# Kurtosis of 1024 rows: loads of changing size, a larger first result batch, another split of the last fourth powers, and the last results with one row per partition

## Chip, cores, metric

The kernel runs on one core of a Trainium2 chip. The metric is the device time of one execution in microseconds. "The span" is the length of a profiled execution; the measured time is about 1.7 us longer (100.4 and 102.1 us for the kernel before). A packet is one entry of the trace's DMA list, here one contiguous piece of a row. A semaphore is a counter on which an engine waits.

## The reference

```python
x = np.random.randn(1024, 8192).astype(np.float32)
mean = np.mean(x, axis=-1, keepdims=True)
std = np.std(x, axis=-1, keepdims=True)
z = (x - mean) / (std + 1e-8)
return (np.mean(z ** 4, axis=-1) - 3).astype(np.float32)     # 1024 results, 4 KB
```

The input is 33.55 MB and is read once. The output is 4 KB.

## The kernel before

The rows go in 16 groups of 64. A row fills two partitions, so a group is a tile of 128 partitions x 4096 values (2 MB). For each group the TensorE transposes and adds 32 blocks (`turn`), the VectorE (DVE) adds the two halves (`reduce`), the TensorE makes the mean of each partition (`mean`), and the ScalarE (ACT) squares the centred values (`square`). The fourth powers are split between ACT (512 columns) and DVE (3584); in the last group 2304 and 1792. The SyncE (SP) issues all loads and stores.

```python
def load(i):                                   # 4 loads of 512 KB a group, all issued by SP
    ...
    for c in range(0, W, CHUNK):               # CHUNK = 1024, W = 4096
        nc.sync.dma_start(out=xt[:, c:c + CHUNK], in_=src[:, c:c + CHUNK])

def second_moment(b):                          # n groups of batch b, R = 64 rows each
    p2 = psfin.tile([n, R], f32, name="p2")    # one partition per group, 64 results in it
    nc.tensor.matmul(p2, lhsT=sa[:, 0:n], rhs=sel, start=True, stop=True)
    ...                                        # rec = 1/p2; rec2 = -rec*rec

def finish(b, rec2):
    ...                                        # p4: the same with the fourth powers (2 matmuls)
    nc.vector.tensor_mul(kr, p4, rec2)
    nc.vector.tensor_scalar_add(kr, kr, -3.0)
    dst = out[b[0] * R:(b[0] + n) * R].rearrange("(g r) -> g r", r=R)
    nc.sync.dma_start(out=dst, in_=kr)         # n packets of 256 B

for i in range(GROUPS):
    turn(i); reduce(i); mean(i); square(i)     # (one line here, four in the kernel)
    if i >= 1: fourth_dve(i - 1, ACT_S4)
    if i < L:  fourth_act(i, ACT_S4)
    if i == LAG_BATCH + 1: finish(batches[0], second_moment(batches[0]))
rec2 = second_moment(batches[1]); rec2l = second_moment(batches[2])
fourth_act(L, LAST_ACT_S4); fourth_dve(L, LAST_ACT_S4)
finish(batches[1], rec2); finish(batches[2], rec2l)
```

The batches are groups 0 to 11, 12 to 14, and 15.

Of the kernel before, what the change touches and what calls it, by code (L numbers as in the profile page):

```python
# [1 line left out]

# [4 lines left out]

f32 = mybir.dt.float32
bf16 = mybir.dt.bfloat16
AO = mybir.AluOpType  # L10
AF = mybir.ActivationFunctionType
P = 128

K = 2
GROUPS = 16
CHUNK = 1024
SLOTS = 12
ACT_S4 = 512
LAST_ACT_S4 = 2304
LAG_BATCH = 12  # L20


@with_exitstack
def kernel(
    ctx: ExitStack,
    tc: tile.TileContext,
    x: bass.AP,
    out: bass.AP,
):
    nc = tc.nc  # L30
    n_rows, n_cols = x.shape
    R = P // K
    W = n_cols // K
    assert n_rows == GROUPS * R
    neg_inv_n = -1.0 / float(n_cols)
    AX = mybir.AxisListType.X

    xpool = ctx.enter_context(tc.tile_pool(name="xpool", bufs=SLOTS))
    const = ctx.enter_context(tc.tile_pool(name="const", bufs=1))
    small = ctx.enter_context(tc.tile_pool(name="small", bufs=4))  # L40
    fin = ctx.enter_context(tc.tile_pool(name="fin", bufs=3))
    psum = ctx.enter_context(tc.tile_pool(name="psum", bufs=2, space=bass.MemoryType.PSUM))
    psfin = ctx.enter_context(tc.tile_pool(name="psfin", bufs=1, space=bass.MemoryType.PSUM))
    ctx.enter_context(tc.manual_schedule())

    warm = const.tile([P, 1], f32, name="warm")
    nc.vector.memset(warm, 0.0)  # L47
    nc.scalar.activation(out=warm, in_=warm, func=AF.Square)  # L48

    ident = const.tile([P, P], f32, name="ident")  # L50
    nc.gpsimd.memset(ident, 1.0)
    nc.gpsimd.affine_select(
        out=ident, in_=ident, pattern=[[-1, P]], base=0,
        channel_multiplier=1, compare_op=AO.is_equal, fill=0.0)
    negcol = const.tile([P, 1], f32, name="negcol")
    nc.gpsimd.memset(negcol, neg_inv_n)

    sel = const.tile([P, R], f32, name="sel")
    nc.gpsimd.memset(sel, neg_inv_n)
    nc.gpsimd.affine_select(  # L60
        out=sel, in_=sel, pattern=[[-K, R]], base=0,
        channel_multiplier=1, compare_op=AO.is_ge, fill=0.0)
    nc.gpsimd.affine_select(
        out=sel, in_=sel, pattern=[[K, R]], base=K - 1,
        channel_multiplier=-1, compare_op=AO.is_ge, fill=0.0)
    one = const.tile([1, 1], f32, name="one")
    nc.gpsimd.memset(one, 1.0)

    batches = [list(range(LAG_BATCH)), list(range(LAG_BATCH, GROUPS - 1)), [GROUPS - 1]]
    where = {}  # L70
    for b in batches:
        n = len(b)
        sa = const.tile([P, 2 * n], f32, name=f"sa{b[0]}")
        sd = const.tile([P, n], f32, name=f"sd{b[0]}")
        for j, i in enumerate(b):
            where[i] = (j, n, sa, sd)

    xts = {}
    tpss = {}
    reds = {}  # L80
    mpss = {}

    def load(i):
        xt = xpool.tile([P, W], f32, name="xt")
        xts[i] = xt
        src = x[i * R:(i + 1) * R, :].rearrange("r (k w) -> (r k) w", k=K)
        for c in range(0, W, CHUNK):
            nc.sync.dma_start(out=xt[:, c:c + CHUNK], in_=src[:, c:c + CHUNK])  # L88

    def turn(i):  # L90
        tps = psum.tile([P, P], f32, name="tps")
        tpss[i] = tps
        for c in range(0, W, P):
            nc.tensor.matmul(tps, lhsT=xts[i][:, c:c + P], rhs=ident,  # L94
                             start=c == 0, stop=c == W - P, is_transpose=True)

    def reduce(i):
        red = small.tile([P, P], f32, name="red")
        reds[i] = red
        nc.vector.tensor_reduce(  # L100
            out=red.rearrange("p (r k) -> p r k", k=K),
            in_=tpss[i].rearrange("p (r k) -> p r k", k=K).unsqueeze(2).to_broadcast([P, R, K, K]),
            op=AO.add, axis=AX)

    def mean(i):
        mps = psum.tile([P, 1], f32, name="mps")
        nc.tensor.matmul(mps, lhsT=reds[i], rhs=negcol, start=True, stop=True)  # L107
        nmu = small.tile([P, 1], f32, name="nmu")
        nc.scalar.copy(nmu, mps)  # L109
        mpss[i] = nmu  # L110

    def square(i):
        j, n, sa, sd = where[i]
        nc.scalar.activation(out=xts[i], in_=xts[i], func=AF.Square, bias=mpss[i],  # L114
                             accum_out=sa[:, j:j + 1])

    def fourth_act(i, c):
        j, n, sa, sd = where[i]
        nc.scalar.activation(out=xts[i][:, :c], in_=xts[i][:, :c], func=AF.Square,  # L119
                             accum_out=sa[:, n + j:n + j + 1])  # L120

    def fourth_dve(i, c):
        j, n, sa, sd = where[i]
        nc.vector.tensor_tensor_reduce(  # L124
            out=xts[i][:, c:], in0=xts[i][:, c:], in1=xts[i][:, c:], scale=1.0, scalar=0.0,
            op0=AO.mult, op1=AO.add, accum_out=sd[:, j:j + 1])


    def second_moment(b):
        j, n, sa, sd = where[b[0]]  # L130
        p2 = psfin.tile([n, R], f32, name="p2")
        nc.tensor.matmul(p2, lhsT=sa[:, 0:n], rhs=sel, start=True, stop=True)  # L132
        rec = fin.tile([n, R], f32, name="rec")
        nc.vector.reciprocal(rec, p2)  # L134
        rec2 = fin.tile([n, R], f32, name="rec2")
        nc.vector.scalar_tensor_tensor(  # L136
            out=rec2, in0=rec, scalar=-1.0, in1=rec, op0=AO.mult, op1=AO.mult)
        return rec2

    def finish(b, rec2):  # L140
        j, n, sa, sd = where[b[0]]
        p4 = psfin.tile([n, R], f32, name="p4")
        nc.tensor.matmul(p4, lhsT=sa[:, n:2 * n], rhs=sel, start=True, stop=False)  # L143
        nc.tensor.matmul(p4, lhsT=sd, rhs=sel, start=False, stop=True)  # L144
        kr = fin.tile([n, R], f32, name="kr")
        nc.vector.tensor_mul(kr, p4, rec2)  # L146
        nc.vector.tensor_scalar_add(kr, kr, -3.0)  # L147
        dst = out[b[0] * R:(b[0] + n) * R].rearrange("(g r) -> g r", r=R)
        nc.sync.dma_start(out=dst, in_=kr)

    L = GROUPS - 1
    for i in range(GROUPS):
        load(i)
    for i in range(GROUPS):
        turn(i)
        reduce(i)
        mean(i)
        square(i)
        if i >= 1:
            fourth_dve(i - 1, ACT_S4)  # L160
        if i < L:
            fourth_act(i, ACT_S4)
        if i == LAG_BATCH + 1:
            finish(batches[0], second_moment(batches[0]))
    rec2 = second_moment(batches[1])
    rec2l = second_moment(batches[2])
    fourth_act(L, LAST_ACT_S4)
    fourth_dve(L, LAST_ACT_S4)
    finish(batches[1], rec2)
    finish(batches[2], rec2l)  # L170


# [1 line left out]
_INS = ['x']  # L174
_OUTS = [((1024,), 'float32')]


# [23 lines left out]
```

## Time and profile before

| | before |
|---|---|
| time, median of 4 runs | 102.06 us (102.01 to 102.17) |
| span | 100.4 us |
| group 15 complete in SBUF | 87.36 us |
| square of group 15 starts | 89.72 us |
| last DVE operation ends | 98.07 us |
| last store: issued, landed | 98.09, 99.26 us |

"Complete" and "landed" are from the trace's list of semaphore increments: each of the up to 16 DMA engines of a transfer adds one when its share is done, and the last counts. The prediction shows the lines of the page and the timeline.

### The profile page before, as it was taken

Reading aid. Unit: us, or ns where it says so; the run is one execution under the profiler, and the core shown is the slowest. Engines: PE = TensorE matmul, PEld = TensorE weight load, DVE = VectorE, ACT = ScalarE, POOL = GpSimd, SP = SyncE. Lnnn points to the kernel's source line nnn. Section 1 sums busy time; section 2 is a strip of 40 time slices with the busy share of each in tenths; the row PEclk is TensorE's granted clock in tenths of the full one; section 3 lists DMA queues with packets and bytes.
Section 4 is the critical chain, followed back from the end, with each engine's and each line's share of the span. In section 5 each row is a group of like instructions: output and inputs, shape, how many; then the busy total and the mean of one; then the engine's idle time right before and its main releaser. Section 6 shows DMA issues by size and latency. Waiting matters only on the chain.

```text
span 100.4 us, 1513 instructions
## 1 busy us (share of the span) xinstructions
PE 73.0 (73%) x562; PEld 63.2 (63%) x562; DVE 69.2 (69%) x61; ACT 77.7 (77%) x82; POOL 1.3 (1%) x11
## 2 busy tenths in 40 slices
PE   0099797979597978888797979797979796940320
PEld 0099697967475858676777767676767695930210
DVE  0000104989792969696979787888878799979770
ACT  5000089999996798989797999898989897999910
POOL 5000000000000000000000000000000000000000
PEclk9999999999999999999999999999999999999555
DMA  1999999999999999999999999999999999100000
GB/s 59 284 374 372 418 418 415 415 405 408 408 413 406 408 415 406 405 410 415 405 410 415 405 410 410 406 405 408 411 410 408 408 408 371 64 0 0 0 0 3
DMA packets 9255, 33.65 MB, mean 335 GB/s; under 512 B 1056, under 2 KB 1056, under 8 KB 9248
## 3 DMA queue, kind: packets, MB, share of 16 engines
q1 hardware_dynamic: 9248, 33.56, 84.7%
q8 instruction: 4, 0.07, 0.3%
q14 instruction: 3, 0.02, 0.1%
HBM read 33.55 MB, written 0.00 MB: 334 GB/s over the span
## 4 chain that ended last, share of the span: by engine, by line
DMA 77%; DVE 8%; ACT 8%; PE 1%; issue 1%; SPq 1%; ACTq 0%; DVEq 0%
DMA xt<-in_x_dram 77%; ACT xt L114 8%; DVE xt L124 6%; DVE rec L134 1%; SPq L88 1%; ACT xt L119 1%; DVE kr L146 1%; DVE red L100 0%; PE p L132 0%; PE p L143 0%; PE mps L107 0%; DVE rec L136 0%; DVE kr L147 0%; PE p L144 0%; ACTq L114 0%
## 5 line engine op out<-in xcount | busy, mean ns | idle before, releaser
L94 PE MATMUL tps<-ident,xt 128*128 128x128 f32 x512 | 67.1, 285 | 8.1 <-DMA xt<-in_x_dram 8.0
L94 PEld LDWEIGHTS tps<-ident,xt 128*128 128x128 f32 x512 | 59.3, 148 | 13.8 <-DMA xt<-in_x_dram 7.7
L124 DVE CUSTOM_DVE_ANT_0 xt<-xt 128x3584 f32<-128x3584 f32 (+1 forms) x16 | 60.3, 3766 | 0.2 <-ACT xt L114 0.2
L114 ACT ACTIVATE xt<-xt,nmu 128x4096 f32<-128x4096 f32 x16 | 59.5, 3718 | 0.9 <-ACT nmu L109 0.3
L100 DVE TENSOR_REDUCE red<-tps 128x128 f32<-128x256 f32 x16 | 6.8, 424 | 26.4 <-PE tps L94 26.4
L109 ACT COPY nmu<-mps 128x1 f32<-128x1 f32 x16 | 2.5, 157 | 15.8 <-PE mps L107 15.6
L107 PEld LDWEIGHTS mps<-negcol,red 128*128 128x128 f32 x32 | 4.8, 188 | 13.3 <-ACT xt L114 9.0
L107 PE MATMUL mps<-negcol,red 128*128 128x1 f32 x32 | 5.7, 247 | 9.9 <-DVE red L100 8.7
L119 ACT ACTIVATE xt<-xt 128x512 f32<-128x512 f32 (+1 forms) x16 | 11.6, 723 | 0.5
L132 PE MATMUL p<-sel,sa 128*12 128x64 f32 (+2 forms) x6 | 0.9, 244 | 3.9 <-ACT xt L114 3.9
L143 PE MATMUL p<-sel,sa 128*12 128x64 f32 (+2 forms) x6 | 1.1, 273 | 2.6 <-DVE kr L146 2.6
L119 ACT ACTIVATION_READ_ACCUMULATOR xt<-xt 128x1 f32 x16 | 3.0, 186 | 0.0
L114 ACT ACTIVATION_READ_ACCUMULATOR xt<-xt,nmu 128x1 f32 x16 | 2.9, 184 | 0.0
L132 PEld LDWEIGHTS p<-sel,sa 128*12 128x12 f32 (+2 forms) x6 | 0.3, 84 | 4.1 <-ACT xt L114 4.1
L143 PEld LDWEIGHTS p<-sel,sa 128*12 128x12 f32 (+2 forms) x6 | 0.5, 101 | 2.9 <-issue 2.9
L134 DVE RECIPROCAL rec<-p 12x64 f32<-12x64 f32 (+2 forms) x3 | 1.6, 543 | 0.5 <-PE p L132 0.5
L48 ACT ACT_TABLE_LOAD x1 | 1.3, 1283 | 0.8 <-PEq L185 0.8
L124 DVE DVE_READ_ACCUMULATOR2_ANT sd<- 128x1 f32 x16 | 1.3, 82 | 0.0
L144 PE MATMUL p<-sel,sd 128*12 128x64 f32 (+2 forms) x6 | 1.1, 281 | 0.0
L146 DVE TENSOR_TENSOR kr<-p,rec 12x64 f32<-12x64 f32 (+2 forms) x3 | 0.6, 211 | 0.7 <-PE p L144 0.6
L136 DVE SCALAR_TENSOR_TENSOR rec<-rec 12x64 f32<-12x64 f32 (+2 forms) x3 | 0.6, 213 | 0.1
L47 DVE MEMSET warm<- 128x1 f32 x1 | 0.1, 59 | 0.9 <-PEq L185 0.9
(14 smaller groups left out, 3.1 us busy)
## 6 DMA issues: line engine op xcount, KB each, us to landing
xt<-in_x_dram SPq DMA_DIRECT2D x64, 512.0 KB, 10.2
out_dram<-kr SPq DMA_DIRECT2D x1, 3.0 KB
out_dram<-kr SPq DMA_DIRECT2D x1, 0.8 KB
out_dram<-kr SPq DMA_DIRECT2D x1, 0.2 KB
```

The lines of the kernel that those rows point to most:

```text
L48: nc.scalar.activation(out=warm, in_=warm, func=AF.Square)
L94: nc.tensor.matmul(tps, lhsT=xts[i][:, c:c + P], rhs=ident, start=c == 0, stop=c == W - P, is_transpose=True)
L100: nc.vector.tensor_reduce(out=red.rearrange("p (r k) -> p r k", k=K), in_=tpss[i].rearrange("p (r k) -> p r k", k=K).unsqueeze(2).to_broad ...
L107: nc.tensor.matmul(mps, lhsT=reds[i], rhs=negcol, start=True, stop=True)
L109: nc.scalar.copy(nmu, mps)
L114: nc.scalar.activation(out=xts[i], in_=xts[i], func=AF.Square, bias=mpss[i], accum_out=sa[:, j:j + 1])
L119: nc.scalar.activation(out=xts[i][:, :c], in_=xts[i][:, :c], func=AF.Square, accum_out=sa[:, n + j:n + j + 1])
L124: nc.vector.tensor_tensor_reduce(out=xts[i][:, c:], in0=xts[i][:, c:], in1=xts[i][:, c:], scale=1.0, scalar=0.0, op0=AO.mult, op1=AO.add, ...
L132: nc.tensor.matmul(p2, lhsT=sa[:, 0:n], rhs=sel, start=True, stop=True)
L134: nc.vector.reciprocal(rec, p2)
L143: nc.tensor.matmul(p4, lhsT=sa[:, n:2 * n], rhs=sel, start=True, stop=False)
L146: nc.vector.tensor_mul(kr, p4, rec2)
```

## The change

The intent was threefold. Larger loads have fewer packets, and finer pieces at the end let the last transposes start early. Results with one row per partition make the last DVE operations one or two elements long. A larger first batch takes more of the finishing work out of the end. With these, the second batch is finished before the last fourth powers instead of after them, and ACT takes 1792 columns of those instead of 2304.

```diff
-CHUNK = 1024
+PIECES = [[4096]] * 7 + [[2048, 2048]] * 5 + [[1536, 1536, 1024]] * 3 + [[1536, 1280, 768, 512]]
-LAST_ACT_S4 = 2304
-LAG_BATCH = 12
+LAST_ACT_S4 = 1792
+LAG_BATCH = 13
...
-        for c in range(0, W, CHUNK):
-            nc.sync.dma_start(out=xt[:, c:c + CHUNK], in_=src[:, c:c + CHUNK])
+        c = 0
+        for w in PIECES[i]:
+            nc.sync.dma_start(out=xt[:, c:c + w], in_=src[:, c:c + w])
+            c += w
...
+        shape = [n, R] if wide else [R, n]
+        nc.tensor.matmul(p2, lhsT=s2 if wide else sel, rhs=sel if wide else s2, ...)
...
+        if n == 1 and not wide:
+            nc.vector.tensor_scalar(out=kr, in0=p4, scalar1=rec2, scalar2=-3.0,
+                                    op0=AO.mult, op1=AO.add)
...
-        dst = out[b[0] * R:(b[0] + n) * R].rearrange("(g r) -> g r", r=R)
+        dst = out[b[0] * R:(b[0] + n) * R]
+        dst = dst.rearrange("(g r) -> g r", r=R) if wide else dst.rearrange("(g r) -> r g", r=R)
         nc.sync.dma_start(out=dst, in_=kr)
...
-            finish(batches[0], second_moment(batches[0]))
-    rec2 = second_moment(batches[1])
-    rec2l = second_moment(batches[2])
+            finish(batches[0], second_moment(batches[0], True), True)
+    rec2 = second_moment(batches[1], False)
+    finish(batches[1], rec2, False)
     fourth_act(L, LAST_ACT_S4)
     fourth_dve(L, LAST_ACT_S4)
-    finish(batches[1], rec2)
-    finish(batches[2], rec2l)
+    rec2 = second_moment(batches[2], False)
+    finish(batches[2], rec2, False)
```

Below, "wide" means 64 results in one partition, stored as one 256 B packet per group; "narrow" means one row per partition, stored as 4 B packets. The batches are now groups 0 to 12 (wide), 13 and 14 (narrow), and 15 (narrow).

More of the change, by code (lines that the diff above doesn't have):

```diff
@@ L126, in fourth_dve, with second_moment @@
             op0=AO.mult, op1=AO.add, accum_out=sd[:, j:j + 1])
-    def second_moment(b):
+    def second_moment(b, wide):
         j, n, sa, sd = where[b[0]]
-        p2 = psfin.tile([n, R], f32, name="p2")
-        nc.tensor.matmul(p2, lhsT=sa[:, 0:n], rhs=sel, start=True, stop=True)
-        rec = fin.tile([n, R], f32, name="rec")
+        shape = [n, R] if wide else [R, n]
+        p2 = psfin.tile(shape, f32, name="p2")
+        s2 = sa[:, 0:n]
+        nc.tensor.matmul(p2, lhsT=s2 if wide else sel, rhs=sel if wide else s2,
+                         start=True, stop=True)
+        rec = fin.tile(shape, f32, name="rec")
         nc.vector.reciprocal(rec, p2)
-        rec2 = fin.tile([n, R], f32, name="rec2")
+        rec2 = fin.tile(shape, f32, name="rec2")
         nc.vector.scalar_tensor_tensor(
@@ L138, in second_moment, with finish @@
         return rec2
-    def finish(b, rec2):
+    def finish(b, rec2, wide):
         j, n, sa, sd = where[b[0]]
-        p4 = psfin.tile([n, R], f32, name="p4")
-        nc.tensor.matmul(p4, lhsT=sa[:, n:2 * n], rhs=sel, start=True, stop=False)
-        nc.tensor.matmul(p4, lhsT=sd, rhs=sel, start=False, stop=True)
-        kr = fin.tile([n, R], f32, name="kr")
-        nc.vector.tensor_mul(kr, p4, rec2)
-        nc.vector.tensor_scalar_add(kr, kr, -3.0)
-        dst = out[b[0] * R:(b[0] + n) * R].rearrange("(g r) -> g r", r=R)
+        shape = [n, R] if wide else [R, n]
+        p4 = psfin.tile(shape, f32, name="p4")
+        for s, (s4, first) in enumerate(((sa[:, n:2 * n], True), (sd, False))):
+            nc.tensor.matmul(p4, lhsT=s4 if wide else sel, rhs=sel if wide else s4,
+                             start=first, stop=not first)
+        kr = fin.tile(shape, f32, name="kr")
+        if n == 1 and not wide:
+            nc.vector.tensor_scalar(out=kr, in0=p4, scalar1=rec2, scalar2=-3.0,
+                                    op0=AO.mult, op1=AO.add)
+        else:
+            nc.vector.tensor_mul(kr, p4, rec2)
+            nc.vector.tensor_scalar_add(kr, kr, -3.0)
+        dst = out[b[0] * R:(b[0] + n) * R]
+        dst = dst.rearrange("(g r) -> g r", r=R) if wide else dst.rearrange("(g r) -> r g", r=R)
         nc.sync.dma_start(out=dst, in_=kr)
```

## The prediction

> **What bounds the kernel now.** The core must read 33.55 MB, and first I asked whether that or the arithmetic sets the end. I read the chain that ended last, the slices, the chain in order of time, the timeline of the last stage, stretches of half a microsecond, and last the trace's lists of DMA packets (start, duration, size) and of semaphore increments by the DMA engines.
>
> ```profile
> DMA 77%; DVE 8%; ACT 8%; PE 1%; issue 1%; SPq 1%; ACTq 0%; DVEq 0%
> ...
> GB/s 59 284 374 372 418 418 415 415 405 408 408 413 406 408 415 406 405 410 415 405 410 415 405 410 410 406 405 408 411 410 408 408 408 371 64 0 0 0 0 3
> ...
> DMA packets 9255, 33.65 MB, mean 335 GB/s; under 512 B 1056, under 2 KB 1056, under 8 KB 9248
> ```
>
> The load is 77% of the chain, and the queue runs near 408 GB/s with no gap from 10 to 85 us. From the semaphore list, the 64 loads of 512 KB complete at a steady 1.279 us each; groups 12, 13, 14 and 15 are complete at 72.14, 77.25, 82.35 and 87.36 us. So the span of 100.4 us is a load up to 87.36 and a tail of 13.0 us. The compute could go faster than the load: with data waiting, squares follow each other by 4.64 us (13.01, 17.65, 22.29 in the timeline), while the load needs 5.1 us a group. That slack of some half a microsecond a group matters below.
>
> ```profile
> 78.77 3.88 DVE L124 CUSTOM_DVE_ANT_0 xt<-xt 128x3584 f32<-128x3584 f32 x1
> ...
> 79.61 3.73 ACT L114 ACTIVATE xt<-xt,nmu 128x4096 f32<-128x4096 f32 x1
> ...
> 82.57 0.54 DVE L134 RECIPROCAL rec<-p 12x64 f32<-12x64 f32 x1
> ...
> 83.82 0.40 DVE L100 TENSOR_REDUCE red<-tps 128x128 f32<-128x256 f32 x1
> ...
> 84.98 3.72 ACT L114 ACTIVATE xt<-xt,nmu 128x4096 f32<-128x4096 f32 x1
> ...
> 89.72 3.71 ACT L114 ACTIVATE xt<-xt,nmu 128x4096 f32<-128x4096 f32 x1
> ...
> 93.98 0.55 DVE L134 RECIPROCAL rec<-p 1x64 f32<-1x64 f32 x1 [0.51 <-PE p L132]
> ...
> 94.71 2.03 DVE L124 CUSTOM_DVE_ANT_0 xt<-xt 128x1792 f32<-128x1792 f32 x1
> ...
> 97.64 0.21 DVE L146 TENSOR_TENSOR kr<-p,rec 1x64 f32<-1x64 f32 x1 [0.55 <-PE p L144]
> ...
> 97.89 0.18 DVE L147 TENSOR_SCALAR kr<-kr 1x64 f32<-1x64 f32 x1
> ...
> 98.09 0.23 SPq L149 DMA_DIRECT2D out_dram<-kr  x1
> ```
>
> These show the last stage. The squares of groups 13, 14, 15 start at 79.61, 84.98, 89.72. The first batch's small DVE work (82.57 to 83.82) holds back the reduction of group 14. Between the last square's end and the last fourth-power pass the DVE does two narrow operations (93.98 to 94.71). After that pass come 1.3 us of matmul and narrow operations, the output issue, and 2.1 us to the end.
>
> **What the Trainium skill says.** (1) "DMA: Bandwidth & Descriptors", section "Why small descriptors are slow (HBM only)": a fixed overhead of about 3 cycles per packet. The trace agrees that there is one and makes it larger: on the load queue a 4 B packet takes 9.5 ns, a 256 B one 17.25, a 4096 B one 159 (mode). A line through the last two gives 0.0369 ns/B (27.1 GB/s an engine) and 7.8 ns a packet. Eight packets and the 4 B semaphore packet make 8 x 158.7 + 9.5 = 1.279 us, just the pace above. (2) "Perfetto Trace Analysis", section "DMA Optimizations": larger transfers saturate better, splitting lets some start sooner. Here the two are traded against each other. (3) "TensorE: Matmul & The Clock Gate", section "What's actually happening": about the first 3.4 us of work run at half the clock. The first turn shows it, and longer: 205 ns from matmul to matmul until about 11 us, 115 ns after. (4) "VectorE: DVE Perf Modes", section "First, the fixed hardware budget": reciprocal is an iterative divide with a repeat count of 8. The trace agrees: 64 elements a partition take 541 ns where another operation of that shape takes 214.
>
> **The change part by part.** *Larger loads.* A row piece of a whole group is 16 KB, contiguous. If it travels as one packet, each costs 7.8 + 604.8 = 612.6 ns. An engine then needs, for a group: whole, 8 x 612.6 + 9.5 = 4.910 us, against 4 x 1.279 = 5.116 now, saving 0.206; halves, 2 x (8 x 310.2 + 9.5) = 4.982, saving 0.134; 1536, 1536, 1024: 2 x (8 x 234.6 + 9.5) + 1.279 = 5.052, saving 0.064; the last about nothing. Sum: 7 x 0.206 + 5 x 0.134 + 3 x 0.064 = 2.30 us, nearly all before group 14. So group 13 is complete at 75.0, group 14 at 80.05 and group 15 at 85.07.
>
> *Coarser starts.* The first turn can begin only with the whole group: at about 9.0 us, not 5.26. It runs cold: about 28 matmuls x 0.205 and 4 x 0.115 = 6.2 us, to 15.2. Before, 1.19 us passed from the turn's end (11.82) to the square, so the first square starts at about 16.4 (13.01 before). From there 13 x 4.64 gives square 13 at 76.7 at the earliest. The data path gives 75.0 + 2.36 (as 77.25 to 79.61 before) = 77.4. Nearly a tie: the slack I noted is spent, and only just suffices. More speed in the load would be worth nothing here.
>
> *The larger first batch, one group later.* Its small DVE work, 1.2 us, moves from before the reduction of group 14 to before that of group 15. From 78.77 in the timeline (the DVE pass that precedes it, 1.52 us after the data of group 13) to 84.98 is 6.21 us. So square 15 cannot start before 80.05 + 1.5 + 6.2 = 87.75. Before it started 89.72 - 82.35 = 7.37 after group 14 was complete, now 7.7: this costs 0.33. The finer last piece (512 columns) gains nothing beyond it, as this path is later.
>
> *The tail.* From square 15 on, before: last DVE end 98.07 - 89.72 = 8.35 us. After: the square's data are ready for DVE after 3.84 (as 17.65 to 21.49); the second batch's four small operations, now one to two elements a partition and about 0.15 each, fall before that and may push it by 0.1. Fourth powers over 2304 columns: 2.03 + 512 x 1.04 ns = 2.56 (slope from the 1792 and 3584 forms, 2.03 and 3.88). The split is better because ACT and DVE now start almost together. Reciprocal and its square for the last batch lie beside the last matmul (0.14 to start, 0.42 for two passes at the clock of 0.5 seen there), then one fused operation of about 0.15. Sum: 3.95 + 2.56 + 0.14 + 0.42 + 0.18 = 7.25 us, saving 1.1.
>
> *Output.* Now 64 rows of 4 B in place of one packet of 256 B. Before, issue to packet took 0.71 us, to completion 1.17, then 1.1 to the end. A few more packets per engine at 9.5 ns are nothing; a longer issue (the output issues of 1 and 12 rows took 0.23 and 0.40) and sixteen completions in place of one are about +0.2, an estimate.
>
> Sum: -2.30 (load) + 0.33 (batch) - 1.1 (tail) + 0.2 (output) = -2.9 us. 102.04 - 2.9 = 99.2. The tie in the compute path (76.7 against 77.4) leaves a hiccup in some group little room; I allow 0.1 and predict **99.3 us**.
>
> **The rivals.** *Packets stay at 4 KB.* If the descriptors are cut there whatever the request, only 34 semaphore packets an engine go (34 x 9.5 ns = 0.3 us), and the time is 102.04 - 0.3 + 0.33 - 1.1 + 0.2 = 101.2. Against it: the instruction fetch in this trace moves packets of 8192 and of 16384 B, so larger ones exist, and an idle 8192 B packet took 307 ns, where my line gives 310. For it: the four 16384 B fetches took 1.03 to 1.1 us each, well above my 0.61 (they ran beside load packets). I give it one chance in five.
>
> *The compute becomes the bound.* Whole-group pieces delay every turn in the first half, and the turn, reduction and mean form a loop of 4.45 us (turns at 12.64 and 17.10) against a load of 4.91. If the first square comes later than I think, by a microsecond, square 13 comes at 77.7, and further delay passes straight to the end: 99.6 to 100.3. For it: the tie. Against it: ACT's 4.64 held whenever data were there, and 12 buffers cannot stall the load (the first 8 transfers cover seven groups and a half).
>
> ```profile
> 85.00:85.50 0.50, 0.50 (x8) 0.50 (x6) 0.50 (x1) 0.50 (x1) 0.00 (x0) 1.00 0.53 208
> 85.50:86.00 0.50, 0.50 (x7) 0.50 (x6) 0.50 (x1) 0.50 (x1) 0.00 (x0) 1.00 0.32 131
> 86.00:86.50 0.50, 0.50 (x7) 0.50 (x6) 0.50 (x1) 0.50 (x1) 0.00 (x0) 1.00 0.23 91
> 86.50:87.00 0.50, 0.50 (x7) 0.50 (x6) 0.50 (x1) 0.50 (x1) 0.00 (x0) 1.00 0.11 42
> ```
>
> *The slowest DMA engine.* The last two columns are the DMA share and GB/s: the load fades over 2 us, so some of the 16 engines finish later, and a transfer counts when all have. If the laggards are slow for another reason than packets (a 1 us instruction fetch on one engine), that part stays; my sum, a difference in packets, already leaves it.
>
> *The output of 4 B writes is slow.* Half a microsecond to one more would give 99.8 to 100.3. Nothing in the profile shows such a write.
>
> **Range and chances.** With large packets 98.7 to 100.2 around 99.3; with 4 KB packets about 101.2. So 98.6 to 101.3. Faster by 2% means under 100.04: 0.8 for large packets, of which some nine in ten end below it, gives 0.72. Slower by 2% would need a new stall of 5 us: 0.02. Within 2%: 0.26.
>
> **What would show each step.** Right: load packets of 16384 and 8192 B; slices near 425 GB/s up to 40 us; the last group complete near 85.1; first square near 16.4; square 13 near 77.4 and square 15 near 87.7, held by the DVE's reduction behind the first batch; last DVE end 7.25 us after that; output packet to end as before. Wrong: only 4096 B packets and 408 GB/s; squares 4.64 us apart right to the end with the load long done; a gap of over 1.5 us between the output's issue and its completion. The prediction fails most likely by packets that stay small.

## More of the kernel before

One more line belongs here, from the waits of the kernel before on SP's queue. Its columns are the total wait in us, how often, and the longest.

```profile
SPq L196 <- DMA out_dram<-kr: 0.9, 1, 0.9
```

At its very end the kernel waits 0.9 us for its stores, the round trip of a small transfer.

## The result, and the profile after

The changed kernel takes **103.9 us** (median of 4 runs, 103.48 to 103.94), the kernel before 102.06. The ratio is 1.017, with a 95% interval of 1.014 to 1.020. Ratios here are the mean time of one kernel's runs over that of the other's in the same rounds, so they are not quite the ratio of the quoted medians. Executions over 1.5% slower than the fastest of the same kernel are left out of the means. A faster kernel was forecast (99.3 us, at most 101.3); this one is slower, by less than 2%.

First the page of the changed kernel: the chain that ended last, then the GB/s in 40 slices of 2.55 us, then the packets.

```profile
DMA 75%; DVE 12%; PE 3%; issue 1%; DVEq 0%
...
GB/s 103 315 411 430 443 443 424 417 430 436 436 417 424 424 414 424 424 411 424 424 420 420 427 417 397 412 424 408 424 415 411 401 130 0 1 0 0 0 0 0
...
DMA packets 4576, 33.64 MB, mean 329 GB/s; under 512 B 730, under 2 KB 730, under 8 KB 2394
```

The load did become faster: 424 to 443 GB/s in the slices from 7.7 to 18 us, half as many packets, and the load ends two slices earlier. (Single slices are rough, as a packet counts whole where it starts; groups 1, 2 and 3 are complete 4.89 us apart, which is 429 GB/s.) But seven slices at the end, some 18 us, hold almost no bytes, where the kernel before has five (12.5 us). Next, the last stage in the timeline (start and length in us, then engine, line, operation and shapes). The last line is the issue of the last store, from the timeline of SP.

```profile
76.72 3.74 ACT L117 ACTIVATE xt<-xt,nmu 128x4096 f32<-128x4096 f32 x1
...
81.57 3.73 ACT L117 ACTIVATE xt<-xt,nmu 128x4096 f32<-128x4096 f32 x1
...
84.88 0.54 DVE L141 RECIPROCAL rec<-p 13x64 f32<-13x64 f32 x1
...
86.13 0.40 DVE L103 TENSOR_REDUCE red<-tps 128x128 f32<-128x256 f32 x1
...
87.29 3.71 ACT L117 ACTIVATE xt<-xt,nmu 128x4096 f32<-128x4096 f32 x1
...
91.21 2.56 DVE L127 CUSTOM_DVE_ANT_0 xt<-xt 128x2304 f32<-128x2304 f32 x1
...
93.69 0.16 DVE L141 RECIPROCAL rec<-p 64x1 f32<-64x1 f32 x1
...
94.24 0.21 DVE L156 TENSOR_SCALAR kr<-p,rec 64x1 f32<-64x1 f32 x1 [0.21 <-PE p L152]
...
94.48 0.49 SPq L163 DMA_DIRECT2D out_dram<-kr  x1
```

The squares of groups 13, 14 and 15 start at 76.72, 81.57 and 87.29 (79.61, 84.98 and 89.72 before), and the last DVE operation ends at 94.45 instead of 98.07. At that point the changed kernel is 3.6 us ahead. Then it has only its last store to do. In stretches of the end (the columns are the length, the busy time of PE, PEld, DVE, ACT and POOL, then clock, DMA share and GB/s) nothing runs:

```profile
95.50:98.40 2.90, 0.00 (x0) 0.00 (x0) 0.00 (x0) 0.00 (x0) 0.00 (x0) 0.50 0.01 0
98.40:101.20 2.80, 0.00 (x0) 0.00 (x0) 0.00 (x0) 0.00 (x0) 0.00 (x0) 0.50 0.00 0
```

And this is the line of the changed kernel that answers to SP's 0.9 us above:

```profile
SPq L210 <- DMA out_dram<-kr: 6.1, 1, 6.1
```

The kernel waits 6.1 us for stores of 768 bytes in all. The packet list says more. The middle batch's 128 packets of 4 B leave the engines between 92.53 and 92.73 us, 7 to 9 ns each; its last engine reports completion (adds one to the semaphore) at 98.38. The last group's 64 packets leave between 95.63 and 95.80, and its 16 engines report one after the other from 96.06 to 101.17 us. So the packets of the last store take under 0.2 us, and their completions arrive over the next five. From the last DVE operation to the end of the span the kernel before needs 100.39 - 98.07 = 2.3 us, the changed one 102.10 - 94.45 = 7.65.

### The profile page after: what moved, and what is told of

It is laid out like the page before. It is cut to its first block, busy times and chain, and to the rows that moved or that the text cites. A ratio compares the mean times of both kernels' runs of the same rounds, so it can differ in the third digit from the quotient of the medians.

```text
span 102.1 us, 1447 instructions
## 1 busy us (share of the span) xinstructions
PE 68.6 (67%) x562; PEld 63.8 (62%) x562; DVE 69.5 (68%) x60; ACT 76.2 (75%) x82; POOL 1.3 (1%) x11
## 4 chain that ended last, share of the span: by engine, by line
DMA 75%; DVE 12%; PE 3%; issue 1%; DVEq 0%
DMA xt<-in_x_dram 75%; DVE xt L127 10%; PE tps L97 2%; PE p L152 1%; DVE rec L141 0%; DVE red L103 0%; DVE kr L159 0%; DVE rec L143 0%; DVE kr L156 0%; DVEq L127 0%; DVE kr L160 0%; DVE sd L127 0%; DVEq L159 0%
## 5 line engine op out<-in xcount | busy, mean ns | idle before, releaser
L97 PE MATMUL tps<-ident,xt 128*128 128x128 f32 x512 | 62.2, 281 | 9.9 <-DMA xt<-in_x_dram 9.8
L152 PE MATMUL p<-sd,sel 128*64 128x2 f32 (+1 forms) x4 | 0.7, 256 | 3.5 <-DVE sd L127 3.5
L152 PEld LDWEIGHTS p<-sd,sel 128*64 128x64 f32 x4 | 0.6, 204 | 3.7 <-DVE sd L127 3.7
L152 PE MATMUL p<-sa,sel 128*64 128x2 f32 (+1 forms) x4 | 0.6, 226 | 1.4 <-ACT xt L122 1.4
L152 PEld LDWEIGHTS p<-sa,sel 128*64 128x64 f32 x4 | 0.5, 170 | 1.5 <-ACT xt L122 1.5
L138 PE MATMUL p<-sa,sel 128*64 128x2 f32 (+1 forms) x4 | 0.6, 231 | 0.4 <-DVE kr L160 0.4
L141 DVE RECIPROCAL rec<-p 13x64 f32<-13x64 f32 (+2 forms) x3 | 0.9, 284 | 0.0
L138 PEld LDWEIGHTS p<-sa,sel 128*64 128x64 f32 x4 | 0.5, 168 | 0.5 <-ACT xt L117 0.5
L143 DVE SCALAR_TENSOR_TENSOR rec<-rec 13x64 f32<-13x64 f32 (+2 forms) x3 | 0.5, 173 | 0.1
```

The lines of the kernel that those rows point to most:

```text
L97: nc.tensor.matmul(tps, lhsT=xts[i][:, c:c + P], rhs=ident, start=c == 0, stop=c == W - P, is_transpose=True)
L138: nc.tensor.matmul(p2, lhsT=s2 if wide else sel, rhs=sel if wide else s2, start=True, stop=True)
L141: nc.vector.reciprocal(rec, p2)
L143: nc.vector.scalar_tensor_tensor(out=rec2, in0=rec, scalar=-1.0, in1=rec, op0=AO.mult, op1=AO.mult)
L152: nc.tensor.matmul(p4, lhsT=s4 if wide else sel, rhs=sel if wide else s4, start=first, stop=not first)
```

## The experiments

Eleven kernels were run, one of them twice, each correct unless it says that its result is wrong.

### Which part costs the time: four runs

**e1_all_wide** undoes the narrow layout alone.

```diff
-    rec2 = second_moment(batches[1], False)
-    finish(batches[1], rec2, False)
+    rec2 = second_moment(batches[1], True)
+    finish(batches[1], rec2, True)
...                                            # and the same for batches[2]
```

> The changed kernel with the last two batches laid out as before (64 results of a group side by side in one partition, stored as 256 B packets); loads, batches and split stay changed. Theory W (the end is 4-byte stores that land one after the other): the last DVE operation comes about 1.0 us later than in the changed kernel (95.4 us in place of 94.45), but issue to completion falls from 6.7 us to about 1.2, span near 97.8, time 99.5. Rival L (the loss has nothing to do with the stores; something later than the DVE holds the end anyway): stays near 103.9.

Measured: 99.27 us (99.10 to 99.47), ratio 0.972 (0.970 to 0.974). The rival fell. The last DVE operation is later than in the changed kernel, and the wait for the stores is gone (timeline, then SP's waits, of this run):

```profile
95.45 0.18 DVE L160 TENSOR_SCALAR kr<-kr 1x64 f32<-1x64 f32 x1
...
SPq L210 <- DMA out_dram<-kr: 0.7, 1, 0.7
```

So the narrow layout finishes the arithmetic 95.63 - 94.45 = 1.2 us sooner and stores its results so slowly that the kernel is 103.9 - 99.3 = 4.6 us slower for it.

**e2_b1_wide** makes only the middle batch wide (the first half of the diff above), so that the last 64 narrow stores are alone.

> The changed kernel with only the middle batch (groups 13 and 14) laid out as before, the last group still stored as 64 rows of 4 B. Theory W with one shared queue (some 44 ns a store, 128 stores of the middle batch then 64 of the last one): the last batch no longer waits behind 128 others, lands about 2.9 us after its packets, time about 101.6. Rival F (such a store has a fixed latency of 5.4 us whatever its size and company): no gain, 104.3.

Measured: 103.97 us (103.94 to 104.36), ratio 1.019. The view of the stores in this run:

```profile
DMA to landing us min/median/max: 6.3/6.3/6.3
```

This view counts from the start of the issue to the last landing, so it holds some 1.3 us that pass before the last packet has left. With no other narrow store about, the 64 packets leave by 96.31 us and have landed at 101.30, 5.0 us later. My first theory, one shared queue of 44 ns a store, fell here: taking away 128 of the 192 stores shortened nothing. Rival F (slow in themselves) still stood.

**e3_b2_wide** is the opposite: the middle batch narrow, the last group wide.

> The changed kernel with only the last group laid out as before (one 256 B packet), the middle batch still 128 stores of 4 B. The middle batch lands near 98.4 us as in the changed kernel and holds the end: span near 99.4, time 101.2 under both theories. They differ in when the last 256 B packet itself completes: W with one shared queue, not before about 97.5 (behind the others); rival F, about 0.5 us after its packet, near 96.6.

Measured: 100.82 us (100.21 to 101.03), ratio 0.987. The middle batch's 128 stores land until 98.21, 5.5 us after their packets, and hold the end. The last group's single packet starts at 95.75 and has landed at 96.10, while the others are still pending. A store is therefore not held up by pending ones elsewhere; again no shared queue.

**e4_before_loads** is the kernel before with only the new load pieces (`PIECES` and the loop over it).

> The kernel before with only the new load pieces. If larger packets pay as in the changed kernel's trace: groups 13, 14, 15 complete near 76, 81, 84.2 us (77.25, 82.35, 87.36 before), the first square at 16.2, the compute then paces (4.64 us a group); square 15 starts near 86.8, end 10.7 us after it as before: span 97.5, time 99.1. Rival (the compute that starts 3 us later eats the gain): square 15 at 88.5 or later, time 100.9 or more.

Measured: 99.18, 99.24 and 99.55 us (one of 100.90 slow), ratio 0.973 (0.971 to 0.975). The first of these lines is the square of group 15, the second the last DVE operation:

```profile
86.96 3.71 ACT L116 ACTIVATE xt<-xt,nmu 128x4096 f32<-128x4096 f32 x1
...
95.19 0.18 DVE L149 TENSOR_SCALAR kr<-kr 1x64 f32<-1x64 f32 x1
```

The loads alone are worth 2.8 us (the mean is 99.32, that of the kernel before in the same rounds 102.09), and the later start of the compute did not eat them.

### The layout by itself: e5_before_narrow

This is the kernel before with `wide=False` for its last two batches (groups 12 to 14, and 15) and nothing else.

```diff
-    rec2 = second_moment(batches[1])
-    rec2l = second_moment(batches[2])
+    rec2 = second_moment(batches[1], False)
+    rec2l = second_moment(batches[2], False)
...                                            # finish(...) likewise
```

> The kernel before with only the new layout of the last two batches (groups 12 to 14: 192 stores of 4 B; group 15: 64), loads and order unchanged. Both stores are issued at the end, near 97 and 97.7 us. If 4 B stores to the same 256 B of memory go one after the other (5.0 us for 64 of them, as in the run with only the middle batch laid out as before): the last lands near 98.3 + 5.2 = 103.5, span 104.5, time 106.2. If the 256 stores all share one queue at 44 ns each: 98 + 11.3, time 112. If the layout costs nothing by itself: near 101.3, as the DVE gets done about 0.7 us sooner.

Measured: 106.77, 107.27 and 107.54 us, ratio 1.050 (1.047 to 1.054). The shared queue of 44 ns a store, which would have given 112, fell a second time. The measured time is a microsecond above what five microseconds from the last packets would give. The profiled execution was slow for another reason (see the last section), so there is no fast trace of this run. In the slow one the last store landed 6.7 us after the start of its issue (245.05 to 251.75), as in the changed kernel (94.48 to 101.17); the expectation had allowed 5.8 (97.7 to 103.5). With 6.7 its own sum gives 107.1, an estimate that would account for the microsecond.

### Why the stores are slow: five runs

All five have the middle batch wide, as e2_b1_wide, and change only where the last group's narrow results go, or how many of them; two of them leave out the first batch's store as well. They are wrong (some results missing or in other places).

**e6_spread** keeps 64 stores from the same 64 partitions and puts them 52 bytes apart.

```diff
+        if b[0] == 0:
+            return
+        if n == 1:
+            dst = out[0:13 * R].rearrange("(r s) -> r s", s=13)[:, 0:1]
         nc.sync.dma_start(out=dst, in_=kr)
```

> As the run with only the middle batch laid out as before, but the last group's 64 results go 52 bytes apart over the first 3328 bytes of the output, and the first batch isn't stored (wrong results on purpose). The same 64 stores of 4 B from the same 64 partitions and 16 engines. Theory S (stores to the same block of memory go one after the other): some 5 stores a block, all landed within about 1.1 us of their packets, time near 99.9. Rival F (a 4 B store is slow in itself, or 64 of them on 16 engines are): again 5.0 us, time 104.

Measured: 99.07 us (98.94 to 99.14), ratio 0.970. The view of the stores in this run:

```profile
DMA to landing us min/median/max: 1.7/1.7/1.7
```

The packets leave by 96.17 and have all landed at 96.53, 0.35 us later. The same number of 4 B stores, from the same partitions, is quick when the addresses lie apart. Rival F fell: neither the size of the store nor the number of them is slow in itself.

**e7_sixteen** stores only the first 16 results, to 64 neighbouring bytes.

```diff
+        if n == 1:
+            dst, kr = dst[0:16], kr[0:16]
         nc.sync.dma_start(out=dst, in_=kr)
```

> As the run with only the middle batch laid out as before, but only the first 16 of the last group's 64 results are stored (48 are missing on purpose): 16 stores of 4 B to 64 neighbouring bytes. Theory S with a cost for each store to a block (5.0 us / 64 = 78 ns): 16 x 78 = 1.25 us and the fixed 0.5, time near 100.7. S with a block of 64 bytes (312 ns a store, four blocks side by side before): again 5.0 us, time 104. Rival F: 5.0 us, time 104.

Measured: 98.85 us (98.83 to 98.99), ratio 0.969. The view of the stores in this run:

```profile
DMA to landing us min/median/max: 1.3/1.3/1.3
```

Landed 0.32 us after the packets: quicker than all three expectations. Sixteen neighbouring stores cost nothing, so a fixed cost per store to a block is wrong as well. That left two ideas: stores beyond some number to one block of memory (B), or stores that one DMA engine repeats within 64 bytes (E; 16 engines report for 64 rows, so each has four. That these four are neighbouring rows is an assumption of the next runs: the packets of the trace carry no engine number).

**e10_permuted** keeps all 64 stores in the same 256 bytes and only permutes them, so that four neighbouring rows, taken to be those of one engine, lie 64 bytes apart.

```diff
+        if n == 1:
+            dst = out[b[0] * R:(b[0] + 1) * R].rearrange("(j e) -> e j", j=4).unsqueeze(2)
         nc.sync.dma_start(out=dst, in_=kr)
```

> As the run with only the middle batch laid out as before: the last group's 64 stores of 4 B go to the same 256 bytes, but in another order (wrong on purpose): the four rows that one DMA engine should hold (neighbouring partitions) go 64 bytes apart, so no engine writes twice within 64 bytes, and each 64 bytes gets 16 stores from 16 engines, as in the run of sixteen. Theory B (too many stores to one 256-byte block, whoever sends them): landed 5.0 us after the packets, time 104. Theory E (stores that follow each other from one engine to the same 64 bytes wait for one another): landed within 0.6 us, time about 99.2.

Measured: 103.76 and 104.07 us, ratio 1.018. The view of the stores in this run:

```profile
DMA to landing us min/median/max: 6.7/6.7/6.7
```

The packets leave by 96.18, landed at 101.42: 5.2 us, as without the permutation. Theory E fell, if neighbouring rows share an engine.

**e11_sixteen_apart** spaces the 64 stores by 16 bytes, so four neighbouring rows fall within 64 bytes and a 256-byte block gets 16.

```diff
+        if b[0] == 0:
+            return
+        if n == 1:
+            dst = out[0:4 * R].rearrange("(r s) -> r s", s=4)[:, 0:1]
         nc.sync.dma_start(out=dst, in_=kr)
```

> As the run of stores 52 bytes apart, but 16 bytes apart: the four stores of one engine fall within one 64 bytes, which no other engine touches; a 256-byte block gets 16 stores (as many as in the run of sixteen). The first batch isn't stored (wrong on purpose). Theory B: 16 a block is harmless, landed within 0.6 us, time about 99.1. Theory E: each engine repeats itself within 64 bytes, landed 1 to 5 us after the packets, time 100 to 104.

Measured: 99.08 and 99.75 us, ratio 0.974. The view of the stores in this run:

```profile
DMA to landing us min/median/max: 1.7/1.7/1.7
```

Landed 0.35 us after the packets. Theory B held; with the same proviso E fell a second time.

**e12_thirtytwo** stores the first 32 results (`dst[0:32], kr[0:32]` in place of 16).

> As the run of sixteen, with the first 32 of the 64 results stored: 128 bytes, two neighbouring stores an engine. Theory B: a cost that grows with the stores to a block, about half of 5.0: landed 2 to 2.5 us after, time about 101. Theory E: one repeat an engine in place of three, about a third: 1.5 us, time about 100.5. If neither, as quick as sixteen: 98.9.

Measured: 100.80 and 101.39 us, ratio 0.991. The view of the stores in this run:

```profile
DMA to landing us min/median/max: 3.2/3.2/3.2
```

Landed 2.2 us after the packets, as theory B expected. The first eight engines report within 0.1 us of each other, the rest in steps of about 0.4 us. The five runs and e2_b1_wide together:

| 4 B stores | apart | in any 256 bytes | last packet to landed |
|---|---|---|---|
| 16 | 4 B | 16 | 0.32 us |
| 64 | 52 B | about 5 | 0.35 us |
| 64 | 16 B | 16 | 0.35 us |
| 32 | 4 B | 32 | 2.2 us |
| 64 | 4 B | 64 | 5.0 us |
| 64, permuted | 4 B | 64 | 5.2 us |

Up to 16 stores into a block cost nothing extra here. If each beyond that costs the same, it is about a tenth of a microsecond: (2.2 - 0.3) / 16 = 0.12 and (5.0 - 0.3) / 48 = 0.10 us; no run lies between 16 and 32. That the block has 256 bytes is the size that fits all rows, not one that a run pinned down. If blocks don't hold each other up, neighbouring powers of two do not fit: with 128 bytes the 64 stores would be two blocks of 32 and land in 2.2 us, and with 512 the stores 16 B apart would be 32 to a block and not land in 0.35. The 128 stores of the middle batch fit it too: they fill two such blocks with 64 each and take 5.5 us, hardly more than 64 stores in one.

One rival is left. If rows are dealt to the 16 engines in turn (row 0 to the first, row 1 to the second, row 16 to the first again), then in all three slow rows of the table an engine stores more than once into one 256-byte block, and in the three quick ones none does. Then it would be the engine that counts after all (within 256 bytes, not within 64 as in E: dealt in turn, the four stores of an engine in e2_b1_wide lie 64 bytes apart and are slow). The run of 32 speaks against it: each engine would have two stores in the block, but eight of the 16 report at once. No run tests it directly.

### A version from what was learnt: e9_one_batch and e13_one_batch_again

This has the large loads, but the first group in four pieces, and one wide batch for all 16 groups at the end, with 2304 of the last columns on ACT.

```diff
-PIECES = [[4096]] * 7 + ...
+PIECES = [[1024] * 4] + [[4096]] * 6 + ...
-LAST_ACT_S4 = 1792
-LAG_BATCH = 13
+LAST_ACT_S4 = 2304
-    batches = [list(range(LAG_BATCH)), list(range(LAG_BATCH, GROUPS - 1)), [GROUPS - 1]]
+    batches = [list(range(GROUPS))]
...                                            # no finish() in the loop, one after it
+    rec2 = second_moment(batches[0], True)
+    finish(batches[0], rec2, True)
```

> A version built from what was learnt: large loads but the first group in four pieces, all 16 groups' results in one batch at the end laid out as before (16 packets of 256 B), no batch in the middle, 2304 columns of the last fourth powers on ACT. Expected: first square near 13 us, square 15 near 86.6 (no batch work ahead of the last reduction), last DVE operation 7.35 us later at 93.95, output as fast as in the kernel before, span 96.4, time 98.0. Rival (the compute path from the batch work was no limit, the load is): square 15 stays at 87.3, time 98.7.

Measured: 98.44, 98.45 and 98.64 us, ratio 0.965 (0.964 to 0.967).

> The version with one batch at the end a second time, for a profile in the fast state (the first one's fell in an execution with a slowed TensorE, 247 us). Time 98.5 as before; first square near 13 us, square 15 near 86.6, last DVE operation near 94.3, end 2.4 us after it.

Measured: 98.17 and 98.35 us, ratio 0.963 (0.959 to 0.966). Timeline of this run: the first two squares, the last one, and the last DVE operation.

```profile
12.41 3.71 ACT L116 ACTIVATE xt<-xt,nmu 128x4096 f32<-128x4096 f32 x1
...
21.84 3.72 ACT L116 ACTIVATE xt<-xt,nmu 128x4096 f32<-128x4096 f32 x1
...
86.84 3.71 ACT L116 ACTIVATE xt<-xt,nmu 128x4096 f32<-128x4096 f32 x1
...
93.84 0.18 DVE L159 TENSOR_SCALAR kr<-kr 16x64 f32<-16x64 f32 x1
```

It beats both kernels, the kernel before by 3.7%. The finer first group did not do what I wanted: the first square comes at 12.41, but the second must wait for a whole second group and starts at 21.84 (20.80 in the changed kernel). From there 14 squares at 4.64 us lead to 86.8, which is where square 15 starts. So this version is bound by the compute from the second group on. Splitting the second group too was not tried.

## Why the prediction was wrong, point by point

**The larger loads: right, and larger than I said.** The packets of 16384, 8192 and 6144 B have most often 611, 309 and 239 ns (234 nearly as often), where the working had 612.6, 310.2 and 234.6. The rival of packets cut at 4 KB fell. Group 15 is complete at 84.22 us; I had 85.07. Most of the difference is in the first two groups: the second is complete at 13.57 us instead of 14.62, where the working allows 0.4 us for two whole groups. The kernel with the new loads alone gained 2.8 us.

**The coarser start: right.** The first square starts at 16.16 (I had 16.4), square 13 at 76.72 (76.7 from the compute, 77.4 from the data). With the faster load it is the compute that sets it, which was the second rival; it cost nothing against the forecast, as square 15 still came early. Some of this is luck. From matmul to matmul it is 213 and 110 ns in the first turn, not 205 and 115, and how long the slow pace lasts differs: 23 of 32 matmuls here, 17 in e4_before_loads with the same loads, where the first square starts at 15.26.

**The larger first batch: right in kind.** Square 15 starts 8.08 us after group 14 is complete (79.21 us), against 7.7 in the working and 7.37 before, and its reduction waits behind the batch's four DVE operations. The step was worked from the data of group 14, but the pace of ACT before it now counted too. Square 15 itself came at 87.29, earlier than my 87.75.

**The tail: right.** From square 15 to the end of the last DVE operation it took 94.45 - 87.29 = 7.16 us; the sum gave 7.25. One reading on the way was loose: a reciprocal of 541 ns beside an operation of 214 shows that it is slower, not that it repeats eight times.

**The output: this step failed.** The term reads "A few more packets per engine at 9.5 ns are nothing; a longer issue [...] and sixteen completions in place of one are about +0.2, an estimate." What the runs showed is 7.65 us from the last DVE operation to the end in place of 2.3, so +5.3. The spans add up with it: square 15 starts 2.43 us earlier, the tail is 1.19 shorter and the output 5.33 longer, together the +1.7 that was measured. The rival on slow 4 B writes had the right mechanism in name, at half a microsecond to one more; it was undersized by a factor of five and more, and given no chance of its own. The prediction did name the sign that came, a gap of over 1.5 us between the output's issue and its completion (it was 6.7), but held small packets in the load for the likeliest way to fail. With the measured term in place of +0.2, the prediction's own sum gives 99.2 - 0.2 + 5.3 = 104.3, near the measured 103.9.

How it came about can be said: I priced the stores by the time their packets take on the engine, where 4 B packets had only ever been seen as semaphore writes, and 256 B ones as results. No trace of the kernel before holds many 4 B writes to neighbouring addresses in memory. The Trainium skill does have a hint that I passed over: "DMA: Bandwidth & Descriptors", section "Specifications", says that below 512 B the engine does a read-modify-write. Such updates of one block would have to take turns, which fits the table above. But a 256 B packet is below 512 B as well and lands within 0.45 us (0.35 in e3_b2_wide), and no run here shows the reading itself, so that this is the cause is argued and not shown. Shown is that how many stores go to neighbouring addresses decides, and not that a store has 4 B, their number in all, or the company of the other batch. Whether the engine that sends them matters depends on how rows are dealt to engines, which no trace shows.

**Where the gain went.** The loads gave 2.8 us (e4_before_loads). Batches, split and loads without the narrow layout gave 99.27 (e1_all_wide), so that batches and split alone are worth next to nothing on top of the loads. Against e1_all_wide the narrow layout saved 1.2 us of arithmetic at the end and added 5.6 us of landing (7.65 us from the last DVE operation to the end, there 97.72 - 95.63 = 2.1). What the last group's narrow layout could have been worth is seen where its stores were made harmless: 98.85 to 99.07 us (e7_sixteen, e6_spread, with wrong results), 0.2 to 0.4 us under e1_all_wide.

## What to carry to other kernels

A store isn't done when its packets have left: for the last transfer of a kernel, look at the landing, and lay out results so that neighbouring addresses leave in one packet, even if the arithmetic before it gets a microsecond longer. A layout that makes DVE operations short by moving results across partitions turns one contiguous store into many tiny ones; price both sides. Large contiguous row pieces pay on a load that bounds the kernel, as long as the compute that starts later keeps up.

## What the Trainium skill lacked or had wrong

- "DMA: Bandwidth & Descriptors" has no word on many small stores to neighbouring addresses: 64 stores of 4 B side by side land 5.0 us after their packets, 32 in 2.2 us, 16 in 0.32 us, and 64 spaced by 16 B or 52 B in 0.35 us.
- The same page, section "Why small descriptors are slow (HBM only)", puts the overhead of a packet at about 3 cycles. The load's queue here gives 7.8 ns each on a line through 256 B (17.25 ns) and 4 KB (159 ns), and 16 KB lie within 2 ns of that line (611 ns). As 32 B take 1.18 ns on it, 7.8 ns are about 6.6 such steps, where the page counts 3.
- The same page, section "Measured (HBM→SBUF, 128 partitions, SWDGE, issued from GpSimd)", advises 1 MiB and more for 75% of peak. A stream of loads from SP is not held to that here: 512 KB each give about 408 GB/s, 94% of the page's own ceiling of 435, and whole groups of 2 MB (one in 4.89 us) 429.
- "TensorE: Matmul & The Clock Gate", section "Seeing it yourself", says that the clock gate has been seen stuck at a quarter for over 50 us. Two executions here look like it and last longer, though no run shows the gate itself: the first runs of e5_before_narrow and e9_one_batch took 254.5 and 247.5 us, with every turn of 32 matmuls at about 13.2 us in place of 3.7 (0.42 us from matmul to matmul in place of 0.11) and ACT's squares unchanged at 3.71. Their clock is given as 1.0, as their traces hold no clock event at all. One such turn of e9_one_batch in the timeline:

```profile
19.61 13.21 PE L96 MATMUL tps<-ident,xt 128*128 128x128 f32 x32
```
